# Panels for the large weights, and one 1024-column split per part in the mixture of experts (two transformer blocks, Trainium2, one core)

## The chip, the cores and the metric

The kernel runs on one core of one Trainium2 chip. The metric is the device time of one execution in microseconds (us). Engines are named as in the profile: PE multiplies matrices (PEld is its weight load), DVE and ACT are the vector and the scalar engine, POOL is GpSimd, SP issues most transfers. A form like `128x512` gives partitions x columns, and `out<-in` what an instruction writes and reads.

## What is computed

One sequence of 256 tokens with 1024 channels goes through two blocks in float32. Block 1 is an RWKV7 layer with a dense feed-forward part, then an attention layer with a mixture of 8 experts (two for each token, hidden width 3584). Block 2 has a mixer and a convolutional feed-forward part over 256 latent and 256 context tokens, and a second mixer with latent keys. The part that the change touches most:

```python
def swiglu(x, w_gate, w_up, w_down):
    return (jax.nn.silu(x @ w_gate) * (x @ w_up)) @ w_down

def moe_swiglu(x, router, w_gate, w_up, w_down):
    logits = (x @ router).astype(jnp.float32)
    top_logits, top_idx = lax.top_k(logits, TOP_K_EXPERTS)
    top_w = jax.nn.softmax(top_logits, axis=-1)
    gates = jnp.sum(jax.nn.one_hot(top_idx, N_EXPERTS, dtype=jnp.float32) * top_w[..., None], axis=-2)
...
    for e in range(N_EXPERTS):
        out = out + gates[..., e:e + 1] * swiglu(x, w_gate[e], w_up[e], w_down[e])
```

The weights of an expert are [1024, 3584] twice and [3584, 1024].

## The kernel before, in words

A product is held to float32 accuracy by splitting both operands into a high part (rounded to fp32r, which PE multiplies fast) and a low part (the rest): high x high, high x low and low x high are summed. A weight comes in **parts** of 128 partitions x 1024 float32 columns (512 KB). `wload` loads each part on SP's queue into a buffer `wraw` (6 of them), lets ACT copy it into `whi` and DVE subtract `whi` from `wraw` into `wlo` (4 buffers of each kind), both in pieces of `HI_N = LO_N = 512` columns. Each engine runs its instructions in one fixed order, which the framework's scheduler makes from the program, and waits at an instruction whose input isn't there. `act` is L242, `tt` L245, `stt` L254, `mm` L257, `tr` L277, the weights' transfer L301.

In the mixture of experts every expert runs over up to 128 of its tokens (`moe_experts`). A **block** is 512 hidden columns of one expert, 56 blocks in all. It has 12 parts: 4 of the gate's weight, 4 of up, and 4 of down (for the block before it). Each part is used in six matmuls of 512 columns, four with `whi` and two with `wlo`; `xg` are the tokens as stationary operand, `hT` the transposed hidden values. Between the parts stand:

- `gt` on ACT (tanh of the gate's sums, from PE), then `gs` twice on DVE (times the gate's sums, then times the up product's sums),
- four transposes of `gs` on PE (`ident,gs`), `hT` on ACT (their high part, from PE) and `hT` on DVE (their low part).

Where an expert ends its result is scaled (`yh`, `yl`) and scattered back (`moe_acc`); once for two experts the tokens are gathered (`xg`).

Before the change a row of gate or up lies in HBM as it is in the input: a part has for each partition two runs of 2048 bytes. A part of 256-column units (in `lin_T`) has four runs of 1024 bytes, and a part of down, or of another 1024-column matrix taken whole, one run of 4096.

Of the kernel before, what the change touches and what calls it, by code (L numbers as in the profile page):

```python
# [35 lines left out]
for _n, _k in VEC_SPECS:  # L36
# [3 lines left out]
# weight groups held for the last token tile; weights loaded before the lent tiles come in; transposed pairs whose  # L40
# scaling VectorE shares; columns per piece of a weight's split
# [7 lines left out]
    "x", "rwkv_w_rkv", "rwkv_w_out", "rwkv_decay_w0", "rwkv_decay_w1", "rwkv_decay_w2", "rwkv_iclr_a1",  # L49
    "rwkv_iclr_a2", "rwkv_gate_g1", "rwkv_gate_g2",  # L50
    "moba_w_k", "moba_w_v", "moba_w_q", "moba_w_o", "ffn_w_gate", "ffn_w_up", "ffn_w_down",
    "moe_router", "moe_w_gate", "moe_w_up", "moe_w_down", "ln_g", "ln_b",
    "ctx_2", "ada_w_2", "ffn_w_up_2", "ffn_w_down_2",
    "ev_w_in_2", "ev_gate_b_2", "ev_ml_norm_g_2", "ev_w_out_2",
    "od_w_dq_2", "od_w_uq_2", "od_w_dkv_2", "od_w_ukv_2", "od_w_o_2",
# [81 lines left out]
def pack(inputs):  # L137
    """Only layout: every vector that goes along partitions is laid out as [128, n]."""
    out = {}
    cols = []  # L140
    for n, k in VEC_SPECS:
        v = np.asarray(inputs[n], np.float32).reshape(k, P)
        cols.append(v.T)
    out["vecs"] = np.ascontiguousarray(np.concatenate(cols, 1))
    for n in RAW:
        out[n] = np.ascontiguousarray(np.asarray(inputs[n]))
    out["rpb"] = np.ascontiguousarray(np.asarray(inputs["ev_rpb_2"])[0].transpose(2, 0, 1))
    out.update(shape_consts()[0])
    return out
# [9 lines left out]
class Wt:  # L159
    """A weight unit on chip: k-tiles of [128, ncol], as high and low parts."""  # L160
# [16 lines left out]
class Act:  # L177
    """Activations with the contraction on partitions: k-tiles of [128, ntok], high and low parts."""
# [5 lines left out]
class Net:  # L184
    def __init__(self, ctx, tc, a):
        self.tc, self.nc, self.a = tc, tc.nc, a
# [11 lines left out]
        # tiles that the next weights are loaded into (None: one of their own)  # L198
# [60 lines left out]
    def mm3(self, out, xh, xl, wh, wl, start, stop):  # L259
        """One contraction step in float32 accuracy: hi*hi + hi*lo + lo*hi."""  # L260
        self.mm(out, xh, wl, start, False)
        self.mm(out, xl, wh, False, False)
        self.mm(out, xh, wh, False, stop)

    def mmk(self, out, ks, xh, xl, wh, wl, first, last):
        """Contraction steps ks in float32 accuracy, the products with the weights' high parts first; the
        activations are the stationary operand. first / last: the group's first and last steps."""
        for k in ks:
            self.mm(out, xh(k), wh(k), k == first, False)
            self.mm(out, xl(k), wh(k), False, False)  # L270
        for k in ks:
            self.mm(out, xh(k), wl(k), False, k == last)
# [6 lines left out]
    def split(self, hi, lo, src):  # L279
        """src as hi + lo, both readable by the fast float32 matmul."""  # L280
# [3 lines left out]
    def rpow(self, out, x, n, mul, add):  # L284
        """out = (x * mul + add) ** -0.5 for an [128, n] tile."""
# [5 lines left out]
    def wload(self, src, nk, ncol):  # L291
        """Loads [nk*128, ncol] by parts of at most 1024 columns of k-tiles and splits them."""
# [66 lines left out]
    def mmT(self, out, w, x, nk, w0, w1):  # L359
        """out [w1 - w0, 256] = w^T x over nk k-tiles, the weights being the stationary operand."""  # L360
# [6 lines left out]
    def lin_T(self, ch, x, nk, src, n, evac, mcol=P):  # L367
        """Channel-major output: for units of 256 columns evac(c0, ntiles, psum [128, ntiles, 256])."""
# [17 lines left out]
    def to_T(self, ch, src, x, nk=KD, scale=None, bias=None, f32=None):  # L386
        """src(tb) token-major [128, nk*128] -> x (channel-major hi/lo), optionally scaled and shifted per channel."""
# [34 lines left out]
    def layer_norm(self, h, gi, out):  # L422
        """In: h[tb] pre-norm sums [128,1024]; out(tb) normalised, ln_g/ln_b row gi = (layer, which)."""
# [154 lines left out]
def wkv(N, st, ch=0):  # L578
    """The delta-rule recurrence in chunks of 64 tokens, two heads (128 channels) at a time; three
    pairs are in flight: one prepares its products, one inverts, one walks over its chunks."""  # L580
# [151 lines left out]
    def walk(pr):  # L732
        # values with the two heads' tokens stacked on partitions
# [52 lines left out]
    def finish(pr):  # L786
        # group norm, bonus and gate; the result is channel-major
# [31 lines left out]
    # (stage, steps, start and length in units of a pair's turn)  # L819
# [11 lines left out]
def rwkv_out(N, st, ch=0):  # L831
    """Output projection, residual and layer norm."""
# [8 lines left out]
    yield from N.lin_tok(ch, x, KD, a["rwkv_w_out"][0], D, evac, late=lambda: None)  # L841
# [29 lines left out]
def ffn_parts(N, ch, x, wa, wg, parts, slots, unit, evac, wdown, late=None):  # L871
    """Runs unit(k, pa, pg, hi, lo) over pairs of 256 columns, then the down product, for each part of the hidden."""
# [20 lines left out]
def ffn_dense(N, st, ch=0):  # L893
    """SwiGLU feed-forward of block 1's first layer, residual and layer norm."""
# [19 lines left out]
    yield from ffn_parts(N, ch, x, a["ffn_w_gate"][0], a["ffn_w_up"][0], (12, 10), (4, 5, 6), unit, evac, a["ffn_w_down"][0],  # L914
# [20 lines left out]
def softmax_part(N, out, p, scale):  # L935
    """out = softmax(scale * p) along the free dimension."""
# [8 lines left out]
def turned(N, ch, S, n):  # L945
    """[128, n * 128] -> its n blocks transposed, for both heads."""
# [17 lines left out]
def moba(N, st, ch=0):  # L964
    """Block 1's attention layer: 256 tokens are one block, so all that stays is causal attention in it."""
# [15 lines left out]
    yield from paced(chain(N.lin_T(ch, x, KD, a["moba_w_q"][0], D, keep(qT)), N.lin_T(ch, x, KD, a["moba_w_k"], D, keep(kT)),  # L981
# [28 lines left out]
    def turn(pr):  # L1010
        # blocks: [keys0, q0], [keys0, q1], [keys1, q1]
# [18 lines left out]
    yield from paced(N.lin_tok(ch, o, KD, a["moba_w_o"][0], D, evac, late=lambda: None), SIDE["moba_out"])  # L1030
# [23 lines left out]
    # rank of each expert's logit (ties: the lower index first, as top_k)  # L1054
# [1001 lines left out]
```

## Time and profile before

| | |
|---|---|
| median of 3 runs | 2950.31 us (2949.16 to 2954.93) |
| span of the profiled execution | 2942.9 us, clock 0.976 (its whole time isn't given apart from the span) |
| PE busy | 2824.4 us, 96% |
| DVE busy | 2279.5 us, 77% |
| ACT busy | 1809.3 us, 61% |
| moved by transfers | 639.16 MB, 217 GB/s over the span |

The span goes from the first to the last instruction; the time also holds what lies around it. Busy time of matmuls is modelled at their ends, so a busy PE can still be waiting for a weight; the waits tell more. The mixture of experts takes about a third of the span, from some 943 to 1950 us. The stretch before it is the rest of block 1 with the parts of block 2 that don't depend on it, the stretch behind it block 2.

### The profile page before, as it was taken

How to read it: one execution, taken by the hardware profiler on the slowest of the kernel's cores; microseconds unless marked ns; L12 is line 12 of the kernel's file. 1: busy time of each engine (PE TensorE's matmuls, PEld its weight loads, DVE VectorE, ACT ScalarE, POOL GpSimd, SP SyncE). 2: the span in 40 equal slices, each digit the busy share in tenths (PEclk: the TensorE clock that was granted, in tenths of full speed). 3: DMA queues.
4: the chain of work that ended last, by engine and by line, in shares of the span. 5: the costliest groups of instructions: out<-in, count | busy, mean ns of one | idle time of the engine just before them, and what ended most of it. 6: DMA issues, size and time to landing. Idle time of an engine off the chain costs nothing. (4 is left out here: it accounts for less than half of the span.)

```text
span 2942.9 us, 46516 instructions
## 1 busy us (share of the span) xinstructions
PE 2824.4 (96%) x16596; PEld 2336.0 (79%) x16596; DVE 2279.5 (77%) x4406; ACT 1809.3 (61%) x3665; POOL 70.5 (2%) x96
## 2 busy tenths in 40 slices
PE   8999989999998999999999999979989999989898
PEld 8677779988866777778777777758978799877898
DVE  7455456568578999999999999977686786876767
ACT  5334345444466878787877878756444665666655
POOL 0001110000000000000000000000000000000000
PEclk9899989999999999999999999989989999999999
DMA  7346646654425999999999999965532356521463
GB/s 246 102 153 208 207 163 194 187 157 140 158 90 158 347 346 340 347 361 330 352 355 344 345 346 358 352 236 171 159 111 87 116 180 192 158 94 44 138 190 125
DMA packets 356247, 639.16 MB, mean 217 GB/s; under 512 B 25733, under 2 KB 152965, under 8 KB 356006
## 3 DMA queue, kind: packets, MB, share of 16 engines
q1 hardware_dynamic: 348768, 625.58, 63.2%
q10 hardware_dynamic: 7238, 10.52, 1.1%
q8 instruction: 133, 2.18, 0.3%
q14 instruction: 108, 0.88, 0.1%
HBM read 634.97 MB, written 1.05 MB: 216 GB/s over the span
## 5 line engine op out<-in xcount | busy, mean ns | idle before, releaser
L245 DVE TENSOR_TENSOR wlo<-wraw,whi 128x512 fp32r<-128x512 f32 (+1 forms) x2181 | 1377.4, 683 | 268.1 <-ACT whi L242 207.5
L242 ACT ACTIVATE whi<-wraw 128x512 fp32r<-128x512 f32 (+1 forms) x2181 | 1216.2, 621 | 452.7 <-PE ps L257 340.2
L257 PE MATMUL ps<-whi,xg 128*128 128x512 f32 x1792 | 498.7, 397 | 1.0 <-ACT whi L242 1.0
L257 PEld LDWEIGHTS ps<-whi,xg 128*128 128x128 f32 x1792 | 327.3, 188 | 84.7 <-ACT whi L242 23.6
L257 PE MATMUL ps<-wlo,xg 128*128 128x512 f32 x896 | 295.4, 398 | 0.0
L257 PE MATMUL ps<-whi,hT 128*128 128x512 f32 x896 | 259.9, 401 | 0.0
L257 PE MATMUL ps<-hT0h,whi 128*128 128x256 f32 (+2 forms) x872 | 215.3, 284 | 3.8 <-ACT whi L242 3.3
L257 PE MATMUL ps<-hT0l,whi 128*128 128x256 f32 (+2 forms) x872 | 215.1, 284 | 0.3 <-DVE hT0l L245 0.3
L257 PEld LDWEIGHTS ps<-wlo,xg 128*128 128x128 f32 x896 | 168.1, 188 | 55.7 <-DVE wlo L245 20.2
L257 PE MATMUL ps<-whi,hid 128*128 128x512 f32 x704 | 193.6, 411 | 9.6 <-DVE cv L254 3.7
L257 PEld LDWEIGHTS ps<-whi,hT 128*128 128x128 f32 x896 | 164.3, 188 | 33.3 <-ACT whi L242 0.6
L257 PEld LDWEIGHTS ps<-hT0h,whi 128*128 128x128 f32 (+2 forms) x872 | 167.0, 192 | 4.9 <-ACT whi L242 3.5
L257 PEld LDWEIGHTS ps<-whi,hid 128*128 128x128 f32 x704 | 133.6, 194 | 45.7 <-issue 13.4
L257 PEld LDWEIGHTS ps<-hT0l,whi 128*128 128x128 f32 (+2 forms) x872 | 167.1, 192 | 1.0 <-DVE hT0l L245 0.5
L257 PE MATMUL ps<-wlo,hT 128*128 128x512 f32 x448 | 167.5, 416 | 0.0
L257 PE MATMUL ps<-hT1h,whi 128*128 128x256 f32 (+1 forms) x504 | 127.9, 290 | 21.3 <-ACT whi L242 21.3
L254 DVE SCALAR_TENSOR_TENSOR cv<-ps,vecs,cv 128x255 f32<-128x255 f32 x264 | 124.6, 478 | 14.1 <-ACT cv L242 12.6
L257 PE MATMUL ps<-hT1l,whi 128*128 128x256 f32 (+1 forms) x504 | 125.9, 286 | 0.2 <-DVE hT1l L245 0.2
L257 PE MATMUL ps<-hT0h,wlo 128*128 128x256 f32 (+2 forms) x872 | 124.1, 283 | 1.6 <-DVE wlo L245 1.5
L257 PEld LDWEIGHTS ps<-hT0h,wlo 128*128 128x128 f32 (+2 forms) x872 | 112.8, 191 | 3.0 <-DVE wlo L245 2.6
L257 PEld LDWEIGHTS ps<-hT1h,whi 128*128 128x128 f32 (+1 forms) x504 | 96.3, 191 | 23.6 <-ACT whi L242 21.7
L257 PEld LDWEIGHTS ps<-wlo,hT 128*128 128x128 f32 x448 | 84.2, 188 | 28.4 <-DVE wlo L245 10.4
(539 smaller groups left out, 4708.6 us busy)
## 6 DMA issues: line engine op xcount, KB each, us to landing
wraw<-moe_w_down SPq DMA_DIRECT2D x224, 512.0 KB, 5.5
wraw<-moe_w_gate SPq DMA_DIRECT2D x222, 512.0 KB, 5.1
wraw<-moe_w_up SPq DMA_DIRECT2D x222, 512.0 KB, 5.5
wraw<-ffn_w_up SPq DMA_DIRECT2D x154, 512.0 KB, 4.0
wraw<-ada_w SPq DMA_DIRECT2D x96, 512.0 KB, 4.0
wraw<-ffn_w_down SPq DMA_DIRECT2D x88, 512.0 KB, 3.7
wraw<-ev_w_in SPq DMA_DIRECT2D x56, 512.0 KB, 3.7
wraw<-rwkv_w_rkv SPq DMA_DIRECT2D x24, 512.0 KB, 6.6
```

The costliest lines, as they stand in the source:

```text
L242: self.nc.scalar.activation(out, in_, f, **kw)
L245: (eng or self.nc.vector).tensor_tensor(out, x, y, op=op)
L254: (eng or self.nc.vector).scalar_tensor_tensor(out, x, s, y, op0=op0, op1=op1)
L257: self.nc.tensor.matmul(out, l, r, start=start, stop=stop)
```

## The change

Two things. First, the host lays out most large weights by **panels**: for each part the 1024 columns of a partition stand together, so that a part has one run of 4096 bytes for each partition (gate, up, the 256-column units, the 512-column units; down of the experts, `ada_w`, `od_w_uq`, `od_w_dkv` and `od_w_ukv` stay). `Pan` finds a part in such a panel. Second, `wload` takes the width of the pieces, and the experts' two calls ask for 1024: one instruction on ACT and one on DVE for each part, where there were two and two. Elsewhere the pieces stay at 512. (Comments and docstrings go too, which changes nothing.)

```diff
+def panel_width(w, nk):
+    return max(1, min(nk, 1024 // w))
+
+def panels(m, w):
+    nk, n = m.shape[0] // P, m.shape[1]
+    per = panel_width(w, nk)
+    m = m.reshape(nk // per, per, P, n // w, w)
+    return np.ascontiguousarray(m.transpose(3, 0, 2, 1, 4).reshape(n // w, nk // per, P, per * w))
+
+class Pan:
...
+    def part(self, k, m, ncol):
+        k += self.r0 // P
+        assert ncol == self.w and k % self.per == 0 and m <= self.per and self.c0 % self.w == 0
+        return self.ap[self.c0 // self.w, k // self.per][:, :m * ncol]
...
-    def wload(self, src, nk, ncol):
+    def wload(self, src, nk, ncol, hn=HI_N, ln=LO_N):
...
-            nc.sync.dma_start(raw[:, :m * ncol].rearrange("p (k c) -> p k c", k=m),
-                              src[k0 * P:(k0 + m) * P].rearrange("(k p) c -> p k c", p=P))
+            if isinstance(src, Pan):
+                nc.sync.dma_start(raw[:, :m * ncol], src.part(k0, m, ncol))
+            else:
+                nc.sync.dma_start(raw[:, :m * ncol].rearrange("p (k c) -> p k c", k=m),
+                                  src[k0 * P:(k0 + m) * P].rearrange("(k p) c -> p k c", p=P))
...
-            for q in range(0, m, HI_N):
-                e = min(q + HI_N, m)
+            for q in range(0, m, hn):
+                e = min(q + hn, m)
                 self.act(hi[:, q:e], r[:, q:e])
-            for q in range(0, m, LO_N):
-                e = min(q + LO_N, m)
+            for q in range(0, m, ln):
+                e = min(q + ln, m)
                 self.tt(lo[:, q:e], r[:, q:e], hi[:, q:e].bitcast(F32), ALU.subtract)
...
-                w = N.wload(wsrc[0, e, k0 * P:(k0 + 4) * P, f0:f0 + 512], 4, 512)
+                w = N.wload(wsrc[k0 * P:(k0 + 4) * P, f0:f0 + 512], 4, 512, 1024, 1024)
...
-            w = N.wload(a["moe_w_down"][0, e, f0 + j2 * 256:f0 + (j2 + 1) * 256, :], 2, D)
+            w = N.wload(a["moe_w_down"][0, e, f0 + j2 * 256:f0 + (j2 + 1) * 256, :], 2, D, 1024, 1024)
```

The new lines shift the numbers of those below: L242, L245, L254, L257, L277 and L301 become L292, L295, L304, L307, L327 and L352 (panels) or L354 (the rest).

ACT's order in a plain block of the experts, before: 12 half pieces stand between gt and hT, and 12 between hT and the next gt.

```order
L242 ACTIVATE gt<-ps 128x512
L242 ACTIVATE whi<-wraw 128x512 x12
L242 ACTIVATE hT_12851<-ps 128x512
L242 ACTIVATE whi<-wraw 128x512 x12
L242 ACTIVATE gt<-ps 128x512
```

The same place after the change:

```order
L292 ACTIVATE gt<-ps 128x512
L292 ACTIVATE whi<-wraw 128x1024 x6
L292 ACTIVATE hT_12379<-ps 128x512
L292 ACTIVATE whi<-wraw 128x1024 x6
L292 ACTIVATE gt<-ps 128x512
```

The 12 pieces are six whole ones; gt and hT stand after the same number of parts as before.

DVE's order in a plain block, before (`gs<-gt,ps` uses gt, `gs<-gs,ps` the up product's sums):

```order
L254 SCALAR_TENSOR_TENSOR gs<-gt,ps 128x512
L245 TENSOR_TENSOR wlo<-wraw,whi 128x512 x7
L254 SCALAR_TENSOR_TENSOR gs<-gs,ps 128x512
L245 TENSOR_TENSOR wlo<-wraw,whi 128x512 x5
L245 TENSOR_TENSOR hT_12852<-ps,hT_12851 128x512
L245 TENSOR_TENSOR wlo<-wraw,whi 128x512 x12
```

And after:

```order
L304 SCALAR_TENSOR_TENSOR gs<-gt,ps 128x512
L295 TENSOR_TENSOR wlo<-wraw,whi 128x1024 x4
L304 SCALAR_TENSOR_TENSOR gs<-gs,ps 128x512
L295 TENSOR_TENSOR wlo<-wraw,whi 128x1024 x2
L295 TENSOR_TENSOR hT_12380<-ps,hT_12379 128x512
L295 TENSOR_TENSOR wlo<-wraw,whi 128x1024 x6
```

The second gs stands after four whole parts, where it stood after three and a half; hT stands after six in both.

PE's order in the down product of a plain block, from its fifth matmul on, before: the transposes stand in two pairs, the second behind the eleventh matmul.

```order
L257 MATMUL ps<-wlo,hT_14049 128x512
L277 MATMUL ps<-ident,gs 128x128 x2
L257 MATMUL ps<-whi,hT_14049 128x512
L257 MATMUL ps<-whi,hT_14050 128x512
L257 MATMUL ps<-wlo,hT_14049 128x512
L257 MATMUL ps<-whi,hT_14049 128x512
L257 MATMUL ps<-whi,hT_14050 128x512
L257 MATMUL ps<-wlo,hT_14049 128x512
L277 MATMUL ps<-ident,gs 128x128 x2
L257 MATMUL ps<-wlo,hT_14049 128x512
L257 MATMUL ps<-whi,hT_14049 128x512
L257 MATMUL ps<-whi,hT_14050 128x512
```

And after, from the fifth matmul on:

```order
L307 MATMUL ps<-wlo,hT_13433 128x512 x2
L307 MATMUL ps<-whi,hT_13433 128x512
L307 MATMUL ps<-whi,hT_13434 128x512
L307 MATMUL ps<-whi,hT_13433 128x512
L307 MATMUL ps<-whi,hT_13434 128x512
L327 MATMUL ps<-ident,gs 128x128 x4
L307 MATMUL ps<-wlo,hT_13433 128x512 x2
L307 MATMUL ps<-whi,hT_13433 128x512
L307 MATMUL ps<-whi,hT_13434 128x512
```

The four transposes stand together, behind the tenth of the down product's 24 matmuls. In the experts' stretch the number of matmuls is the same; outside of it the rows of PE, DVE, ACT and POOL don't change but for line numbers.

## Rows read from the trace of the kernel before

**Rows 1.** Windows, experts: busy us (count) of PE, PEld, DVE, ACT, POOL; PEclk, DMA share, GB/s

```profile
1400.00:1450.00 50.00, 50.00 (x218) 38.62 (x218) 47.14 (x78) 40.65 (x76) 0.00 (x0) 1.00 0.99 361
```

**Rows 2.** Waits from 960 to 1900 us: total us, times, longest

```profile
ACT hT L242 <- PE ps L277: 87.6, 51, 2.9
ACT gt L242 <- PE ps L257: 65.0, 48, 1.9
PEld ps L257 <- DVE wlo L245: 29.0, 100, 0.4
...
PEld ps L257 <- ACT whi L242: 22.6, 86, 0.7
```

**Rows 3.** Tile gt: ns min/median/max, first and last start

```profile
L242 ACT ACTIVATE gt<-ps x56: 577/598/602, 942.6 to 1929.0; 128x512 f32<-128x512 f32 x56
```

**Rows 4.** Timeline of ACT, three gt in a row: start us, us, [idle before]

```profile
1424.40 0.60 ACT L242 ACTIVATE gt<-ps 128x512 f32<-128x512 f32 x1 [1.51 <-PE ps L257]
...
1441.95 0.60 ACT L242 ACTIVATE gt<-ps 128x512 f32<-128x512 f32 x1 [1.78 <-PE ps L257]
...
1460.70 0.60 ACT L242 ACTIVATE gt<-ps 128x512 f32<-128x512 f32 x1 [1.62 <-PE ps L257]
```

**Rows 5.** Timeline behind gt in a plain block, all engines

```profile
1406.95 0.60 ACT L242 ACTIVATE gt<-ps 128x512 f32<-128x512 f32 x1 [1.03 <-PE ps L257]
...
1407.44 1.14 ACT L242 ACTIVATE whi<-wraw 128x512 fp32r<-128x512 f32 x2
1407.58 0.69 DVE L254 SCALAR_TENSOR_TENSOR gs<-gt,ps 128x512 f32<-128x512 f32 x1 [0.66 <-ACT gt L242]
...
1408.12 0.30 PEld L257 LDWEIGHTS ps<-whi,xg 128*128 128x128 f32 x2 [0.27 <-ACT whi L242]
...
1408.19 2.64 DVE L245 TENSOR_TENSOR wlo<-wraw,whi 128x512 fp32r<-128x512 f32 x4
...
1409.53 0.19 PEld L257 LDWEIGHTS ps<-wlo,xg 128*128 128x128 f32 x1 [0.36 <-DVE wlo L245]
...
1409.86 0.62 PE L257 MATMUL ps<-whi,xg 128*128 128x512 f32 x2
```

**Rows 6.** Timeline behind hT in the same block

```profile
1415.83 0.60 ACT L242 ACTIVATE hT<-ps 128x512 fp32r<-128x512 f32 x1 [0.69 <-PE ps L277]
...
1416.33 3.75 ACT L242 ACTIVATE whi<-wraw 128x512 fp32r<-128x512 f32 x7
1416.46 0.69 DVE L245 TENSOR_TENSOR hT<-ps,hT 128x512 fp32r<-128x512 f32 x1
...
1417.04 0.89 PEld L257 LDWEIGHTS ps<-whi,hT 128*128 128x128 f32 x4
1417.07 3.09 DVE L245 TENSOR_TENSOR wlo<-wraw,whi 128x512 fp32r<-128x512 f32 x5
...
1418.41 0.19 PEld L257 LDWEIGHTS ps<-wlo,hT 128*128 128x128 f32 x1 [0.25 <-DVE wlo L245]
...
1418.75 1.08 PE L257 MATMUL ps<-whi,xg 128*128 128x512 f32 x4
```

**Rows 7.** Tile xm1h, the same two forms at 1024 columns: ns min/median/max

```profile
L242 ACT ACTIVATE xm1h<-xm x2: 1047/1048/1048, 25.5 to 29.7; 128x1024 fp32r<-128x1024 f32 x2
L245 DVE TENSOR_TENSOR xm1l<-xm,xm1h x2: 1209/1209/1209, 28.4 to 32.0; 128x1024 fp32r<-128x1024 f32 x2
```

**Rows 8.** Groups by form, 960 to 1900 us: busy us, mean ns | idle before

```profile
L245 DVE TENSOR_TENSOR wlo<-wraw,whi 128x512 fp32r<-128x512 f32 x1244 | 769.8, 683 | 10.2 <-ACT whi L242 9.1
L242 ACT ACTIVATE whi<-wraw 128x512 fp32r<-128x512 f32 x1246 | 680.7, 622 | 31.4 <-DMA wraw<-moe_w_gate 6.7 <-PE ps L257 5.9 <-DMA wraw<-moe_w_down 4.7
```

**Rows 9.** The page's transfers: KB each, us from issue to landing

```profile
wraw<-moe_w_down SPq DMA_DIRECT2D x224, 512.0 KB, 5.5
...
wraw<-moe_w_up SPq DMA_DIRECT2D x222, 512.0 KB, 5.5
```

**Rows 10.** Waits from 0 to 940 us, the high parts' for transfers

```profile
ACT whi L242 <- DMA wraw<-rwkv_w_rkv: 1.3, 2, 0.9
```

More of the change, by code (lines that the diff above doesn't have):

```diff
@@ L48, with __init__, __getitem__ @@
 RAW = [
-    "x", "rwkv_w_rkv", "rwkv_w_out", "rwkv_decay_w0", "rwkv_decay_w1", "rwkv_decay_w2", "rwkv_iclr_a1",
+    "x", "rwkv_decay_w0", "rwkv_decay_w1", "rwkv_decay_w2", "rwkv_iclr_a1",
     "rwkv_iclr_a2", "rwkv_gate_g1", "rwkv_gate_g2",
[L51 to L55, printed above, removed]
-]
+    "moe_router", "moe_w_down", "ln_g", "ln_b",
+    "ctx_2", "ada_w_2", "ev_gate_b_2", "ev_ml_norm_g_2",
+    "od_w_uq_2", "od_w_dkv_2", "od_w_ukv_2",
+]
+PANELS = [
+    ("p_r", "rwkv_w_rkv", (0, 0), (0, 1024), 256), ("p_k", "rwkv_w_rkv", (0, 1), (0, 1024), 256),
+    ("p_v", "rwkv_w_rkv", (0, 2), (0, 1024), 512), ("rwkv_w_out", "rwkv_w_out", (0,), (0, 1024), 512),
+    ("moba_w_q", "moba_w_q", (0,), (0, 1024), 256), ("moba_w_k", "moba_w_k", (), (0, 1024), 256),
+    ("moba_w_v", "moba_w_v", (), (0, 1024), 512), ("moba_w_o", "moba_w_o", (0,), (0, 1024), 512),
+    ("ffn_w_gate", "ffn_w_gate", (0,), (0, 2816), 256), ("ffn_w_up", "ffn_w_up", (0,), (0, 2816), 256),
+    ("ffn_w_down", "ffn_w_down", (0,), (0, 1024), 512),
[8 rows of a table added]
+]
+for _n in ("moe_w_gate", "moe_w_up"):
+    PANELS += [(f"{_n}{e}", _n, (0, e), (0, FFE), 512) for e in range(NE)]
+def panel_width(w, nk):
[6 more added lines that the diff above has]
+class Pan:
+    def __init__(self, ap, w, nk, r0=0, c0=0):
+        self.ap, self.w, self.nk, self.per, self.r0, self.c0 = ap, w, nk, panel_width(w, nk), r0, c0
+    def __getitem__(self, s):
+        r, c = s if isinstance(s, tuple) else (s, slice(None))
+        return Pan(self.ap, self.w, self.nk, self.r0 + (r.start or 0), self.c0 + (c.start or 0))
+    def part(self, k, m, ncol):
+        k += self.r0 // P
+        assert ncol == self.w and k % self.per == 0 and m <= self.per and self.c0 % self.w == 0
+        return self.ap[self.c0 // self.w, k // self.per][:, :m * ncol]
 def shape_consts():
@@ L146, in pack @@
         out[n] = np.ascontiguousarray(np.asarray(inputs[n]))
+    for n, src, i, (c0, c1), w in PANELS:
+        out[n] = panels(np.asarray(inputs[src])[i][:, c0:c1], w)
     out["rpb"] = np.ascontiguousarray(np.asarray(inputs["ev_rpb_2"])[0].transpose(2, 0, 1))
@@ L185, in __init__ @@
     def __init__(self, ctx, tc, a):
-        self.tc, self.nc, self.a = tc, tc.nc, a
+        self.tc, self.nc, self.a = tc, tc.nc, dict(a)
+        for n, _, _, _, w in PANELS:
+            self.a[n] = Pan(a[n], w, a[n].shape[1] * (a[n].shape[3] // w))
         ep = ctx.enter_context
@@ L840, in evac @@
         N.stt(o, o, ALPHA, p[:, :ncol], ALU.mult, ALU.add)
-    yield from N.lin_tok(ch, x, KD, a["rwkv_w_out"][0], D, evac, late=lambda: None)
+    yield from N.lin_tok(ch, x, KD, a["rwkv_w_out"], D, evac, late=lambda: None)
     N.layer_norm(lambda tb: h[:, tb * D:(tb + 1) * D], (0, 0), lambda tb: h[:, tb * D:(tb + 1) * D])
@@ L913, in evac @@
             N.tt(o, o, p[:, :ncol], ALU.add)
-    yield from ffn_parts(N, ch, x, a["ffn_w_gate"][0], a["ffn_w_up"][0], (12, 10), (4, 5, 6), unit, evac, a["ffn_w_down"][0],
+    yield from ffn_parts(N, ch, x, a["ffn_w_gate"], a["ffn_w_up"], (12, 10), (4, 5, 6), unit, evac, a["ffn_w_down"],
                          lambda: None)
@@ L980, in vevac @@
         N.act(v[:, tb * D + c0:tb * D + c0 + ncol], p[:, :ncol])
-    yield from paced(chain(N.lin_T(ch, x, KD, a["moba_w_q"][0], D, keep(qT)), N.lin_T(ch, x, KD, a["moba_w_k"], D, keep(kT)),
+    yield from paced(chain(N.lin_T(ch, x, KD, a["moba_w_q"], D, keep(qT)), N.lin_T(ch, x, KD, a["moba_w_k"], D, keep(kT)),
                            N.lin_tok(ch, x, KD, a["moba_w_v"], D, vevac)), SIDE["moba_in"])
@@ L1029, in evac @@
         N.stt(q, q, ALPHA, p[:, :ncol], ALU.mult, ALU.add)
-    yield from paced(N.lin_tok(ch, o, KD, a["moba_w_o"][0], D, evac, late=lambda: None), SIDE["moba_out"])
+    yield from paced(N.lin_tok(ch, o, KD, a["moba_w_o"], D, evac, late=lambda: None), SIDE["moba_out"])
     N.layer_norm(lambda tb: h[:, tb * D:(tb + 1) * D], (1, 0), lambda tb: h[:, tb * D:(tb + 1) * D])
@@ L1423, in evac @@
             N.tt(o, o, p[:, :ncol], ALU.add)
-    up = a["ffn_w_up_2"][l]
+    up = a[f"ffn2_up{l}"]
     row = []
-    yield from ffn_parts(N, ch, x, up[:, 0:FF], up[:, FF:2 * FF], parts, hslots, unit, evac, a["ffn_w_down_2"][l],
+    yield from ffn_parts(N, ch, x, up[:, 0:FF], up[:, FF:2 * FF], parts, hslots, unit, evac, a[f"ffn2_down{l}"],
                          lambda: row.extend(gate_row(N, st, ch, l, 1, r)))
@@ L1475, in even_proj @@
     nc, a = N.nc, N.a
-    w = a["ev_w_in_2"][0]
     qo = N.slot(S["qo"], f"nq_mlo{ch}")
@@ L1507, in conv @@
         N.ts(o, o, 0.5 * (128.0 ** -0.5 if k < 4 else 1.0))
-    yield from N.lin_T(ch, x, KD, w[:, 1536:2560], 1024, conv)
-    wg = N.wload(w[:, 3584:3600], KD, 16)
+    yield from N.lin_T(ch, x, KD, a["ev_qk"], 1024, conv)
+    wg = N.wload(a["ev_g"], KD, 16)
     gb = N.sm(1, "gateb")
@@ L1902, in evac @@
         N.act(ql.rearrange("p (n t) -> p n t", n=2), p)
-    yield from paced(N.lin_T(ch, x, KD, N.a["od_w_dq_2"][0], 256, evac), pace)
+    yield from paced(N.lin_T(ch, x, KD, N.a["od_w_dq_2"], 256, evac), pace)
     lat = mla_down(N, ch, x)
```

25 lines of the change are left out of this document (12 added, 13 removed), and 8 rows, old and new, of the table PANELS.

## The prediction

> **What bounds the kernel now.** I read the profile from coarse to fine: the page, the windows of 50 us, the groups of instructions by form, the waits, and then the timeline of one block, where the waits can be put in order.
>
> The page says that PE is busy for 96% of the span. The weights of the experts (the stretch from about 943 to 1950 us) are where the change alters instructions, so I read that stretch by itself. In a window of it all four resources look full [rows 1]: PE busy 50 of 50 us, DVE 47.1, ACT 40.7, the DMA engines at a share of 0.99 with 361 GB/s. Any of them could pass for the bound, and the shares do not decide it. The waits do [rows 2]. In 940 us ACT waits 87.6 us for the transposes ahead of hT and 65.0 us for the gate's sums ahead of gt: it stands idle for PE, it is not late. PE's weight loads wait 29.0 us for DVE's low parts (100 times) and 22.6 us for ACT's high parts (86 times), about 1 us in each of the 52 blocks of that window. So PE is the bound of a block, and what it loses, it loses to hand-overs at two places, not to a full engine.
>
> The block is the unit of the sum. gt runs once in a block, 56 times from 942.6 to 1929.0 us [rows 3], a mean distance of 986.4 / 55 = 17.93 us. Listing all 55 distances I count 35 of 17.6 us or less ("plain" below) and 20 of 18.65 to 19.99, in which an expert's result is combined or the next pair's tokens are gathered. One of each: 17.55 us from 1424.40, 18.75 us from 1441.95 [rows 4].
>
> **The first place, behind gt** [rows 5]. ACT is idle 1.03 us until PE ends the gate's sums, runs gt at 1406.95, and only then goes on to the high part of the next weight part: two 512-column pieces from 1407.44, 1.14 us for both, so the first is there at about 1408.06. PE's load takes it at 1408.12, after 0.27 us of waiting. DVE runs gs (from 1407.58) and begins the low pieces at 1408.19; PE waits 0.36 us for the second and loads it at 1409.53; PE's next part begins at 1409.86. **The second place, behind hT** [rows 6]. ACT waits 0.69 us for the transposes, runs hT at 1415.83, high pieces from 1416.33, 7 in 3.75 us. PE loads the first at 1417.04, with no wait. DVE's low pieces start at 1417.07, behind its own hT (1416.46); PE waits 0.25 us for the second at 1418.41, and the next part begins at 1418.75. At both places the pieces are handed on by halves, and PE starts on the first half while the second is being made.
>
> **The change, part by part.**
>
> (a) One instruction for a part. A 128x1024 copy to fp32r on ACT takes 1048 ns and a subtraction of this form on DVE 1209 ns [rows 7], against 622 and 683 ns for the halves [rows 8]. Seen as work this saves. Back to back, ACT's 7 pieces in 3.75 us are (3.75 - 0.62) / 6 = 0.522 us each and DVE's 5 in 3.09 us are (3.09 - 0.68) / 4 = 0.602 each [rows 6], so that a part costs 1.04 and 1.20 us; if the long forms overlap their neighbours by as much (0.10 and 0.08 us, an estimate), a part will cost 0.95 and 1.13. That is 0.08 us of DVE a part, 0.9 us in a block of 12, some 50 us over 672 parts. It is worth nothing where the engine then waits for PE, as both do in every block.
>
> Seen as a hand-over it costs. The first half no longer comes after 0.62 us; nothing comes before 1.05 us, and DVE can't start while ACT is on the second half. At the first place: ACT starts at 1407.44 as before, because gt stands after the same number of parts in its order; the whole high part is there at 1408.49, and PE's load goes at 1408.54 instead of 1408.12. DVE's subtraction starts at about 1408.55 instead of 1408.19 and ends 1.21 later, at 1409.76. In the rows a load follows its piece by some 0.06 us, so the first low load goes at 1409.82. From the second low load to the next part it is 0.33 us in the rows (1409.53 to 1409.86), and the first load lies one matmul ahead of that, 0.23 us (50 us over 218 in the window of [rows 1]): the next part begins 0.56 us behind it, at 1410.38 instead of 1409.86: **+0.52 us**.
>
> At the second place the same chain gives 1416.33 + 1.05 = 1417.38 for the high part, 1417.44 + 1.21 = 1418.65 for the low, 1418.71 + 0.34 + 0.23 = 1419.28 for the next part instead of 1418.75: +0.53, if hT stays where it is. It does not: PE's order after the change has the four transposes together behind ten of the down product's 24 matmuls, where the last pair stood behind eleven, so hT can start 0.23 us earlier against PE, and ACT, which waited 0.69 us there, can use all of it: **+0.30 us**. The ends are 0.53, if DVE's queue or gs keeps hT where it is, and 0, if ACT and DVE, having gained on PE at the first place, bring hT further forward still. A plain block then costs 0.82 us more (0.52 to 1.05); 35 of them 29 us (18 to 37).
>
> In the other 20 blocks other work on PE, one to two microseconds of it (the distances), lies among the parts and can cover a late hand-over. The nearest rows are the plain blocks at one end and no cost at the other: 0 to 1.05 us each, 0 to 21 us. I take +0.2 each, 4 us, because the extra instructions stand on ACT's and DVE's queues as well and delay them by about what they give PE.
>
> The Trainium skill weighs both sides of this edit in one section ("Perfetto Trace Analysis", Optimizing Scalar/DVE Operations): larger operations improve throughput if the engine is saturated, and if engines are not saturated but cause bubbles on others, "breaking up instructions may allow work to be completed sooner". By the first half the edit would gain, by the second it loses; the idle 1.03 and 0.69 us put this kernel into the second.
>
> (b) Panels. Gate and up weights now come in 4096-byte runs for each partition, as the down weights always have. From issue to landing a part of up takes 5.5 us in its 2048-byte runs and a part of down 5.5 us in its 4096-byte runs [rows 9]: the row shows nothing to be had from longer runs here. ACT waited for gate and down transfers 6.7 and 4.7 us in 940 us [rows 8], and behind such waits PE mostly had parts in hand. So 0, with 11.4 us as the most. Outside of the experts the order of PE, DVE, ACT and POOL is unchanged row by row, and the only wait of a high part for a weight is 1.3 us at the start [rows 10]: -1 us, with 0 and -1.3 as ends. Fewer packets on SP's queue delay nobody: no instruction moves past another there.
>
> **Sum.** 29 + 4 + 0 - 1 = +32 us. The view shows one execution's span, 2942.9 us; the median of the runs is 2950.31, 7.4 us more, which lies around the span and which I leave as it is. 2942.9 + 32 = 2974.9 of span, 2950.3 + 32 = **2982 us**, 1.1% slower. Its own ends are 18 - 11 - 1 = +6 and 37 + 21 = +58 us, 2956 to 3008; both need all unknowns on one side, so I count 2964 to 3002 as its range. What a measurement of this kernel can tell from no change is 0.2%, 5.9 us.
>
> **Rivals.**
>
> *DVE and ACT set the pace after all.* If a block of 12 parts were bound by DVE (12 x 1.20 + 3 x 0.61 for gs, gs and hT = 16.3 of 17.5 us), the saved 0.9 us would show, up to the 1 us that PE waits: half of it in 55 blocks is -25 us, **2925 us**. For it speaks DVE's 47.1 of 50 us; against it the 0.66 us that DVE stands idle for gt ahead of gs in the very block [rows 5], and that 12 x 0.08 us can't be used before the gate's sums are done. 0.06.
>
> *The transfers set the pace.* A block needs 12 x 512 KB = 6.29 MB, at 361 GB/s 17.4 us, just what it takes. If longer runs freed ACT's waits, 11.4 us go: **2939 us**. For it: the share of 0.99. Against it: the equal landing times, and a queue that is full because SP issues whenever a buffer comes free. The Trainium skill ("Perfetto Trace Analysis", DMA Optimizations) says that going from 2 KB to 4 KB transfers can improve throughput dramatically when DMA-bound; by it this rival would hold. 0.05.
>
> *The buffers swallow it.* Four high and four low buffers let ACT and DVE run ahead of PE; if they were two parts ahead at each place, the late first half would be covered and the time stay at **2950 us**. It decides itself by how many parts stand between the wait for PE and PE's need: at the first place it is one (six matmuls, 1.4 us), which gt, one long copy and one long subtraction (0.5 + 1.05 + 1.21) exceed. 0.07.
>
> **How the numbers follow.** Slower by the hand-over 0.82, no change 0.07, transfers 0.05, engines 0.06. Faster is 0.11, the same 0.07, slower 0.82. The time is that of the likeliest. The range takes the likeliest's own and reaches down to the case of no change: 2950 to 3002; it leaves out the two faster cases and the likeliest's tails, together under 2 in 10.
>
> **What would show it.** gt to gt in plain blocks 18.2 to 18.5 us instead of 17.5; whi 1048 and wlo 1209 ns, 672 of each; PE's loads waiting in the same stretch some 80 to 95 us for ACT and DVE instead of 52, at the first part behind gt and behind hT; the DMA share down to about 0.94 with unchanged bytes; the stretches before 940 us as they were. Wrong it would be if plain blocks stay at 17.5 (the buffers), or fall toward 16.8 with ACT's waits for transfers or DVE's for nothing gone; a gain before 940 us would show that I priced the panels too low.

## The result, and the profile after

The changed kernel takes 2981.82 us (median of 4 runs, 2978.59 to 2986.0) beside 2952.62 us for the kernel before: a ratio of 1.0105, 95% interval 1.0088 to 1.0122. 2982 was forecast, inside a range of 2950 to 3002. The span of the profiled execution is 2976.8 us, 33.9 us longer than before, at the same clock of 0.976.

The window of 50 us that stood ahead of the prediction [rows 1], now of the kernel after (busy us and count of PE, PEld, DVE, ACT, POOL; PEclk, DMA share, GB/s):

```profile
1400.00:1450.00 50.00, 48.88 (x211) 37.48 (x211) 43.77 (x42) 34.26 (x38) 0.00 (x0) 1.00 0.93 342
```

211 matmuls where there were 218. DVE and ACT have less to do (43.8 and 34.3 us), the transfers are less dense (0.93 and 342 GB/s), and PE, which was busy for the whole window, is so for 48.9 us and gets less done: everything has more room but the hand-over. The waits from 960 to 1930 us, again about 52 blocks (total us, times, longest):

```profile
ACT hT L292 <- PE ps L327: 114.6, 49, 3.2
ACT gt L292 <- PE ps L307: 97.7, 48, 2.9
...
PEld ps L307 <- DVE wlo L295: 44.1, 90, 0.7
PEld ps L307 <- ACT whi L292: 36.0, 88, 0.7
DVE wlo L295 <- ACT whi L292: 35.0, 118, 1.0
...
PE ps L307 <- ACT whi L292: 9.4, 36, 0.3
```

The waits of PE's loads for split weights were 51.6 us [rows 2]; the two rows here make 80.1, and with the wait of the matmuls themselves it is 89.5. ACT and DVE wait longer for PE than before, so the saved work turned into idle time. DVE waiting for the high part, 35.0 us, was 9.1 [rows 8]: it has to stand by while ACT makes the half it doesn't need yet. gt in the experts (first and last start), and three of them on ACT's timeline:

```profile
L292 ACT ACTIVATE gt<-ps x56: 578/600/604, 945.4 to 1963.3; 128x512 f32<-128x512 f32 x56
```

```profile
1422.54 0.60 ACT L292 ACTIVATE gt<-ps 128x512 f32<-128x512 f32 x1 [2.62 <-PE ps L307]
...
1440.76 0.60 ACT L292 ACTIVATE gt<-ps 128x512 f32<-128x512 f32 x1 [2.77 <-PE ps L307]
...
1459.01 0.60 ACT L292 ACTIVATE gt<-ps 128x512 f32<-128x512 f32 x1 [1.62 <-PE ps L307]
```

From first to last it is 1017.96 us instead of 986.41: +31.5 of the +33.9 lie between them. A plain block takes 18.22 to 18.25 us here, 17.45 to 17.55 before [rows 4].

The first place, behind the gt at 1440.76 (timeline of all engines), to be held against [rows 5]:

```profile
1441.26 3.89 ACT L292 ACTIVATE whi<-wraw 128x1024 fp32r<-128x1024 f32 x4
1441.39 0.69 DVE L304 SCALAR_TENSOR_TENSOR gs<-gt,ps 128x512 f32<-128x512 f32 x1 [1.23 <-ACT gt L292]
...
1442.34 2.36 DVE L295 TENSOR_TENSOR wlo<-wraw,whi 128x1024 fp32r<-128x1024 f32 x2 [0.25 <-ACT whi L292]
1442.36 0.76 PEld L307 LDWEIGHTS ps<-whi,xg 128*128 128x128 f32 x4 [0.70 <-ACT whi L292]
...
1443.62 0.30 PEld L307 LDWEIGHTS ps<-wlo,xg 128*128 128x128 f32 x2 [0.49 <-DVE wlo L295]
...
1444.19 0.39 PE L307 MATMUL ps<-whi,xg 128*128 128x512 f32 x1
```

From gt to the start of PE's next part it is 1444.19 - 1440.76 = 3.43 us; before it was 1409.86 - 1406.95 = 2.91. PE's load waits 0.70 us for the high part, then 0.49 for the low one, where the waits were 0.27 and 0.36: **+0.52 us**, the forecast's figure. The second place, behind hT, to be held against [rows 6]:

```profile
1431.68 0.60 ACT L292 ACTIVATE hT<-ps 128x512 fp32r<-128x512 f32 x1 [1.58 <-PE ps L327]
...
1432.17 3.89 ACT L292 ACTIVATE whi<-wraw 128x1024 fp32r<-128x1024 f32 x4
...
1433.26 2.36 DVE L295 TENSOR_TENSOR wlo<-wraw,whi 128x1024 fp32r<-128x1024 f32 x2 [0.26 <-ACT whi L292]
1433.28 0.76 PEld L307 LDWEIGHTS ps<-whi,hT 128*128 128x128 f32 x4 [0.20 <-ACT whi L292]
...
1434.54 0.30 PEld L307 LDWEIGHTS ps<-wlo,hT 128*128 128x128 f32 x2 [0.50 <-DVE wlo L295]
...
1435.11 0.62 PE L307 MATMUL ps<-whi,xg 128*128 128x512 f32 x2
```

3.43 us from hT to the next part, 2.92 before: +0.51 counted from hT. The whole block grew by 18.22 - 17.45 = 0.77, so after +0.52 at the first place 0.25 is left for the second: hT comes 0.26 us earlier against PE. The distances between the two say the same: from gt to hT it was 1415.83 - 1406.95 = 8.88 us and is now 9.14, only 0.26 more, and from hT to the next gt it was 8.57 and is now 9.08, the 0.51. The two new forms (mean ns) and two rows of transfers (KB, us from issue to landing):

```profile
L295 DVE TENSOR_TENSOR wlo<-wraw,whi 128x1024 fp32r<-128x1024 f32 x623 | 728.9, 1221 | 36.4 <-ACT whi L292 35.0 <-PE ps L307 0.3
L292 ACT ACTIVATE whi<-wraw 128x1024 fp32r<-128x1024 f32 x623 | 622.7, 1054 | 38.7 <-DMA wraw<-moe_w_down 10.4 <-PE ps L307 9.6 <-DMA wraw<-moe_w_gate 6.5
```

```profile
wraw<-moe_w_down SPq DMA_DIRECT2D x224, 512.0 KB, 5.4
...
wraw<-moe_w_up SPq DMA_DIRECT2D x222, 512.0 KB, 5.3
```

1054 and 1221 ns, as the two other tiles had shown [rows 7]. Up lands after 5.3 us in its 4096-byte runs and took 5.5 in 2048-byte ones [rows 9]; gate, with the same change of layout, lands after 5.2 and took 5.1, and down, which didn't change, 5.4 and 5.5, so these differences are of the size of the scatter.

### The profile page after: what moved, and what is told of

It reads as the page before. It is cut to its first block, busy times and chain, and to the rows that moved or that the text cites. A ratio compares the mean times of both kernels' runs of the same rounds, so it can differ in the third digit from the quotient of the medians.

```text
span 2976.8 us, 45225 instructions
## 1 busy us (share of the span) xinstructions
PE 2840.0 (95%) x16596; PEld 2340.8 (79%) x16596; DVE 2246.9 (75%) x3734; ACT 1748.4 (59%) x2993; POOL 69.6 (2%) x96
## 3 DMA queue, kind: packets, MB, share of 16 engines
HBM read 634.97 MB, written 1.05 MB: 214 GB/s over the span
## 5 line engine op out<-in xcount | busy, mean ns | idle before, releaser
L295 DVE TENSOR_TENSOR wlo<-wraw,whi 128x512 fp32r<-128x512 f32 (+2 forms) x1513 | 1333.0, 920 | 300.0 <-ACT whi L292 235.0
L292 ACT ACTIVATE whi<-wraw 128x512 fp32r<-128x512 f32 (+2 forms) x1513 | 1153.6, 812 | 459.1 <-PE ps L307 348.0
L307 PE MATMUL ps<-whi,xg 128*128 128x512 f32 x1792 | 491.5, 396 | 9.9 <-ACT whi L292 9.9
L307 PEld LDWEIGHTS ps<-whi,xg 128*128 128x128 f32 x1792 | 331.7, 188 | 100.4 <-ACT whi L292 28.9
L307 PE MATMUL ps<-wlo,xg 128*128 128x512 f32 x896 | 284.1, 398 | 2.5
L307 PE MATMUL ps<-whi,hT 128*128 128x512 f32 x896 | 246.8, 397 | 0.0
L307 PE MATMUL ps<-hT0h,whi 128*128 128x256 f32 (+2 forms) x872 | 215.6, 285 | 3.8 <-ACT whi L292 3.3
L307 PE MATMUL ps<-hT0l,whi 128*128 128x256 f32 (+2 forms) x872 | 215.5, 284 | 0.3 <-DVE hT0l L295 0.3
L307 PEld LDWEIGHTS ps<-wlo,xg 128*128 128x128 f32 x896 | 162.4, 188 | 53.6 <-DVE wlo L295 21.6
L307 PE MATMUL ps<-whi,hid 128*128 128x512 f32 x704 | 190.5, 406 | 10.9 <-DVE cv L304 4.1
L307 PEld LDWEIGHTS ps<-whi,hT 128*128 128x128 f32 x896 | 164.9, 188 | 45.0 <-ACT whi L292 9.1
L307 PEld LDWEIGHTS ps<-hT0h,whi 128*128 128x128 f32 (+2 forms) x872 | 167.3, 192 | 4.9 <-ACT whi L292 3.5
L307 PEld LDWEIGHTS ps<-hT0l,whi 128*128 128x128 f32 (+2 forms) x872 | 167.4, 192 | 1.1 <-DVE hT0l L295 0.5
L307 PEld LDWEIGHTS ps<-whi,hid 128*128 128x128 f32 x704 | 131.5, 191 | 46.1 <-issue 13.9
L307 PE MATMUL ps<-wlo,hT 128*128 128x512 f32 x448 | 149.9, 416 | 4.7 <-DVE wlo L295 1.9
L307 PE MATMUL ps<-hT1h,whi 128*128 128x256 f32 (+1 forms) x504 | 132.5, 297 | 19.5 <-ACT whi L292 19.5
L304 DVE SCALAR_TENSOR_TENSOR cv<-ps,vecs,cv 128x255 f32<-128x255 f32 x264 | 124.9, 478 | 14.1 <-ACT cv L292 12.6
L307 PE MATMUL ps<-hT1l,whi 128*128 128x256 f32 (+1 forms) x504 | 130.2, 293 | 0.2 <-DVE hT1l L295 0.2
L307 PE MATMUL ps<-hT0h,wlo 128*128 128x256 f32 (+2 forms) x872 | 124.5, 285 | 1.1 <-DVE wlo L295 1.0
L307 PEld LDWEIGHTS ps<-hT1h,whi 128*128 128x128 f32 (+1 forms) x504 | 99.9, 198 | 22.2 <-ACT whi L292 20.2
L307 PEld LDWEIGHTS ps<-hT0h,wlo 128*128 128x128 f32 (+2 forms) x872 | 113.6, 192 | 2.2 <-DVE wlo L295 1.7
L292 ACT ACTIVATE hT<-ps 128x512 fp32r<-128x512 f32 x56 | 33.5, 598 | 122.1 <-PE ps L327 122.1
```

Of the source, the lines that this page charges most:

```text
L292: self.nc.scalar.activation(out, in_, f, **kw)
L295: (eng or self.nc.vector).tensor_tensor(out, x, y, op=op)
L304: (eng or self.nc.vector).scalar_tensor_tensor(out, x, s, y, op0=op0, op1=op1)
L307: self.nc.tensor.matmul(out, l, r, start=start, stop=stop)
```

## Experiments

The theory: the loss comes from handing on whole parts at the two places where ACT and DVE, held up by PE's sums, have just one part of PE's work as cover; the layout and the amount of work on ACT and DVE have no share in it. Rivals: the transfers, the throughput of the engines, and the wide forms by themselves. Every ratio is to the kernel before on the same chip. Some of the edits change the scheduler's order too: in the experts `panels_only` has PE's, ACT's and DVE's order of before and `wide_only` that of after; for others it is said where it matters. The blocks named plain below are the 30 distances of gt from the sixth on that were 17.6 us or less before; their mean was 17.49 us before and is 18.27 after.

**Panels without the wide pieces** (`panels_only`):

```diff
-                w = N.wload(wsrc[k0 * P:(k0 + 4) * P, f0:f0 + 512], 4, 512, 1024, 1024)
+                w = N.wload(wsrc[k0 * P:(k0 + 4) * P, f0:f0 + 512], 4, 512, 512, 512)
...
-            w = N.wload(a["moe_w_down"][0, e, f0 + j2 * 256:f0 + (j2 + 1) * 256, :], 2, D, 1024, 1024)
+            w = N.wload(a["moe_w_down"][0, e, f0 + j2 * 256:f0 + (j2 + 1) * 256, :], 2, D, 512, 512)
```

> Panels as in the change, but the experts' parts split in 512-column pieces again. Every engine's order is then that of before. Theory (the hand-over of a whole part costs, the layout nothing): 2950 to 2953 us, plain blocks 17.45 to 17.6 us, PE's loads waiting about 52 us in the experts. Rival (the new transfers or their source cost something in the experts): plain blocks above 17.7 us and the time toward 2965 or more. The first gt came 2.8 us later after the change; if the panels are the reason it does so here too.

2945.55 us, a little below the 2950 to 2953 expected; ratio 0.999 (0.9976 to 1.0004); plain blocks 17.48 us. The layout alone can't be told from no change. At the start rT, the first product's result, begins at 23.9 us, and at 25.0 in the kernel before (two rows of ACT, before and with panels; first and last start):

```profile
L242 ACT ACTIVATE rT<-ps x4: 573/577/580, 25.0 to 40.7; 128x512 f32<-128x512 f32 x4
```

```profile
L292 ACT ACTIVATE rT<-ps x4: 575/576/577, 23.9 to 39.5; 128x512 f32<-128x512 f32 x4
```

That would be the microsecond of the forecast, but one pair of executions doesn't show it: in the ten profiled executions with panels rT begins between 23.6 and 25.5 us, in the three with the old layout between 25.0 and 26.5. gt comes first at 941.75 us here, so its 2.8 us of delay in the profile after isn't the panels'.

**The wide pieces in the old layout** (`wide_only`), the kernel before with the new arguments of `wload` and

```diff
-                w = N.wload(wsrc[0, e, k0 * P:(k0 + 4) * P, f0:f0 + 512], 4, 512)
+                w = N.wload(wsrc[0, e, k0 * P:(k0 + 4) * P, f0:f0 + 512], 4, 512, 1024, 1024)
...
-            w = N.wload(a["moe_w_down"][0, e, f0 + j2 * 256:f0 + (j2 + 1) * 256, :], 2, D)
+            w = N.wload(a["moe_w_down"][0, e, f0 + j2 * 256:f0 + (j2 + 1) * 256, :], 2, D, 1024, 1024)
```

> Layout of before, the experts' parts split in one 1024-column instruction on ACT and one on DVE. Theory: as the change, 2980 to 2985 us, plain blocks 18.2 to 18.4 us. Rival (panels and width both carry a share): in between, near 2966 us.

2980.48 us, ratio 1.0108 (1.0088 to 1.0128); plain blocks 18.28 us, PE's loads waiting as in the changed kernel. The whole loss is the width's.

**Only the low part whole** (`hi512_lo1024`) and **only the high part whole** (`hi1024_lo512`), with panels; the calls' last two arguments become, for the first and the second,

```diff
-4, 512, 1024, 1024)
+4, 512, 512, 1024)
...
-4, 512, 1024, 1024)
+4, 512, 1024, 512)
```

> Panels; ACT's high part in halves, DVE's low part whole. By the chain the low part is the later one at both places: DVE must wait for both halves (0.52 + 0.62 = 1.14 us, against 1.05 whole), so halving the high part alone brings nothing: 18.2 to 18.5 us for a plain block, 2980 to 2988 us. Rival (PE waits for the high part first): most of the loss comes back, 2955 to 2965 us.

> Panels; ACT's high part whole, DVE's low part in halves. DVE starts 0.36 us late at both places but hands on by halves, so PE's next part is late by 0.36 to 0.37 us at each, 0.73 a plain block without the transposes' earlier place (PE's order is that of before here): about 18.1 us, 2970 to 2978 us. Rival (only DVE's width matters): 2950 to 2956 us.

2989.19 us, ratio 1.0137 (1.0117 to 1.0157), and 2978.34 us, ratio 1.0102 (1.0082 to 1.0123), a shade above what was expected of each; plain blocks 18.48 and 18.22. Halving only the first step of the chain is worse than not halving at all: the interval of its ratio overlaps a little with those of the kernels with both whole, but its plain blocks, 18.40 to 18.55 us, all lie above theirs, 18.19 to 18.38. PE's waits with only the low part whole (waits from 960 to 1930 us here, and in the next rows):

```profile
PEld ps L307 <- DVE wlo L295: 61.5, 133, 1.0
DVE wlo L295 <- ACT whi L292: 48.2, 117, 1.2
...
PEld ps L307 <- ACT whi L292: 24.5, 74, 0.5
```

ACT's first half lets PE begin early (24.5 us of waits, 36.0 with both whole), but DVE needs both halves, which take longer than one whole copy, and PE pays at the low part (61.5). With only the high part whole it is the other way round:

```profile
PEld ps L307 <- ACT whi L292: 45.0, 89, 0.7
PEld ps L307 <- DVE wlo L295: 33.7, 94, 1.0
```

Each width costs its own step, and the two don't add up: the whole loss is there with either one. Nor is the new place of the transposes on PE, which came with the wide pieces, needed for a loss: with only the high part whole they stand in two pairs as before, and a plain block still loses 0.74 us on average, shared by the two places (one block: from gt to hT 9.22 us, to the next gt 8.93; before 8.88 and 8.57):

```profile
1401.72 0.60 ACT L292 ACTIVATE gt<-ps 128x512 f32<-128x512 f32 x1 [1.10 <-PE ps L307]
...
1410.94 0.60 ACT L292 ACTIVATE hT<-ps 128x512 fp32r<-128x512 f32 x1 [2.51 <-PE ps L327]
...
1419.87 0.60 ACT L292 ACTIVATE gt<-ps 128x512 f32<-128x512 f32 x1 [1.71 <-PE ps L307]
```

**gt later, wide pieces kept** (`gt_later_wide`). The first five distances of gt after the change are 0.00 to 0.27 us longer than before, the next ones 0.85 to 0.94. Counted in ACT's order, gt stands two to four parts behind the gate's in these first blocks, and from then on one (two in the second block of each expert's end, after the change). In the first blocks ACT isn't late but ahead, waiting for PE to free a buffer (ACT in the third block of the kernel after):

```profile
975.44 0.58 ACT L292 ACTIVATE gt<-ps 128x512 f32<-128x512 f32 x1
975.91 1.05 ACT L292 ACTIVATE whi<-wraw 128x1024 fp32r<-128x1024 f32 x1
977.26 1.06 ACT L292 ACTIVATE whi<-wraw 128x1024 fp32r<-128x1024 f32 x1 [0.29 <-PE ps L307]
```

So gt is put behind the third part of up everywhere, two parts later than in a plain block (`his`, which `wload` now fills, holds the last copy of each part; `issue_after` makes the scheduler queue what is inside it behind the instruction named):

```diff
-        N.act(t, ws[0], AF.Tanh, scale=0.5)
+        with N.tc.issue_after(N.his[-2].ins):
+            N.act(t, ws[0], AF.Tanh, scale=0.5)
```

> The changed kernel (panels, 1024-column pieces) with gt queued on ACT behind the third part of up instead of the first; nothing else is forced. Theory (one part between the wait for PE and PE's need is too little for a whole-part hand-over; the first blocks, in which gt stands two or more parts later, lost nothing): the loss at the first place goes and the old waits there with it, plain blocks 17.4 to 17.7 us, 2948 to 2962 us. Rival (wide instructions cost by themselves, or DVE is late behind the later gs): plain blocks stay at 18.2 us, 2975 us or more.

2950.66 us, ratio 1.0014 (1.0004 to 1.0024); plain blocks 17.52 us on average. Nearly all of the loss is gone with the wide pieces in place. ACT no longer waits for PE at gt (1.0 us in all, 97.7 before this edit), and PE's loads wait 43.1 instead of 80.1 us (waits from 960 to 1900 us, again about 52 blocks):

```profile
PEld ps L308 <- DVE wlo L296: 29.7, 64, 0.7
...
PEld ps L308 <- ACT whi L293: 13.4, 55, 0.9
...
ACT gt L293 <- PE ps L308: 1.0, 2, 0.8
```

**hT later alone** (`hT_later_wide`), the changed kernel with

```diff
-        N.split(hT[0], hT[1], pt)
+        with N.tc.issue_after(N.his[-1].ins):
+            N.split(hT[0], hT[1], pt)
```

> The changed kernel with hT alone queued one part later on ACT and DVE, gt left one part behind the gate's. Theory by the chain: the second place's loss (0.25 to 0.3 us a plain block) and its old wait go, the first place's 0.5 stays: plain blocks 17.7 to 18.0 us, 2962 to 2974 us. Rival: all of the loss stands behind gt, 2978 us or more.

2963.94 us, ratio 1.005 (1.0031 to 1.007); plain blocks 17.85 to 18.02. From gt to hT a plain block keeps the 9.14 us of the changed kernel, and from hT to the next gt it takes 8.72 instead of 9.08: the move gives back at the second place alone. **Both** (`both_later_wide`):

> As the run before, and hT on ACT and DVE queued behind the last part of the down product. Theory: no hand-over stands within one part of PE any more, plain blocks like the first ones of before (17.15 to 17.25 us), 2932 to 2945 us, faster than before in spite of the wide pieces. Rival: the second place isn't a cost of its own, same time as the run before; or later hT delays gs and the next block, slower than it.

2933.47 us, ratio 0.9943 (0.9931 to 0.9956), faster than the kernel before with the very pieces that made it slower. The distances of gt wander here (plain ones 16.15 to 18.02 us, 16.94 on average, where 17.15 to 17.25 was expected), so the whole stretch says more. The two moves nearly add: from the changed kernel's ratio of 1.0105 the one takes 0.0091, the other 0.0055, both 0.0162. **Both with halves** (`both_later_halves`), the same two edits on `panels_only`:

> The same two moves with panels and 512-column pieces. Theory: where the hand-over is covered the width of the pieces doesn't matter: within 0.3% of the run before. Rival (DVE's or ACT's work counts once PE no longer waits): slower than the wide one by up to 0.9 us a block, 50 us.

2926.17 us, ratio 0.993 (0.9916 to 0.9943): the lowest median of all, though its interval overlaps with that of the wide one. Where the hand-over is covered the width makes 0.13%, if anything, and not 1.05; PE's transposes stand together with the wide pieces and in two pairs with the halves, which may have a share in that difference. From the first gt of the experts to the last it is 970.8 us with wide pieces and 969.6 with halves, and was 986.4 before (first and last start, wide and halves):

```profile
L293 ACT ACTIVATE gt<-ps x56: 577/582/603, 945.2 to 1916.0; 128x512 f32<-128x512 f32 x56
L293 ACT ACTIVATE gt<-ps x56: 576/580/599, 944.2 to 1913.8; 128x512 f32<-128x512 f32 x56
```

**One part less of delay for gt** (`both_later_gt_one_less`):

```diff
-        with N.tc.issue_after(N.his[-2].ins):
+        with N.tc.issue_after(N.his[-3].ins):
             N.act(t, ws[0], AF.Tanh, scale=0.5)
```

> Panels, 512-column pieces, hT one part later, gt behind the second part of up instead of the third. Theory: two parts between are cover enough for halves (0.5 + 0.62 + 0.68 us against 2.7 us of PE), and DVE's gs comes sooner, so that buffers come free sooner and fewer waits for transfers arise: 2918 to 2928 us. Rival: the cover is too thin again, 2930 us or more.

2931.04 us, ratio 0.9941 (0.9921 to 0.996): above the 2918 to 2928 expected and not to be told from the one before; the hoped-for gain isn't there.

**The old layout where transfers count most** (`both_later_old_layout`): the same two edits on the kernel before. In `both_later_halves` PE's loads hardly wait for splits, and what comes up instead is ACT waiting for transfers (waits from 960 to 1900 us):

```profile
ACT whi L293 <- DMA wraw<-moe_w_down: 21.5, 38, 1.5
...
ACT whi L293 <- DMA wraw<-moe_w_gate: 19.5, 26, 1.6
...
ACT whi L293 <- DMA wraw<-moe_w_up: 15.8, 33, 1.5
...
PEld ps L308 <- DVE wlo L296: 10.3, 35, 0.4
```

> The layout of before (2048-byte runs for gate and up), 512-column pieces, gt and hT queued later as in both_later_halves: every engine has the same order as there, only the runs of the transfers differ. There ACT waits for transfers some 58 us in the experts, so if longer runs are ever worth something it is here. Theory (parts of both layouts land equally fast): within 0.3%, 2922 to 2934 us. Rival (2048-byte runs are slower once transfers are next to the bound): 2940 us or more.

2929.44 us, ratio 0.9925 (0.9907 to 0.9942): the same, and ACT waits as long for transfers (58 us from 960 to 1930 us, 59 with panels). Runs of 4096 bytes instead of 2048 bring nothing measurable even there.

**Pieces of 256** (`pieces_256`), with panels:

```diff
-4, 512, 1024, 1024)
+4, 512, 256, 256)
...
-2, D, 1024, 1024)
+2, D, 256, 256)
```

> Panels, pieces of 256 columns on both engines. If only the hand-over counted it would gain on before (first piece 0.2 us earlier), about 2940 us. But DVE's 256-column form takes some 0.42 us (0.34 back to back, by the fixed share seen at 512), 1.38 us a part, 16.6 us a block and 18.4 with gs, gs and hT: DVE becomes the bound and plain blocks take 18.3 to 18.6 us, 2990 to 3010 us. The order that the scheduler makes differs in places too.

2982.94 us, ratio 1.0108 (1.0092 to 1.0124); plain blocks 18.16 us, both below what was expected (2990 to 3010 and 18.3 to 18.6). This is the case in which an engine does set the pace (window of the kernel with 256-column pieces, where DVE is the third pair of numbers, and the largest wait from 960 to 1930 us):

```profile
1450.00:1500.00 50.00, 48.77 (x204) 35.52 (x202) 49.77 (x139) 43.41 (x135) 0.00 (x0) 1.00 0.94 329
```

```profile
PEld ps L307 <- DVE wlo L295: 67.8, 187, 1.1
```

DVE is busy 49.8 of 50 us (49.6 on average from 1000 to 1950 us, 46.9 in the kernel before) and PE waits for the low part. One of DVE's chains of 28 such pieces took 9.47 us:

```profile
1450.59 9.47 DVE L295 TENSOR_TENSOR wlo<-wraw,whi 128x256 fp32r<-128x256 f32 x28
```

With 0.42 us for one, that is (9.47 - 0.42) / 27 = 0.335 us apiece, 1.34 a part; with the three others (gs, gs and hT, 0.61 each as in the prediction) a block needs 17.9 us of DVE.

## Why the prediction was right, step by step

**The bound of a block** was read rightly from the waits and not from the shares. Four resources were near full, and of these the transfers and DVE were cleared by `panels_only`, `both_later_old_layout` and `both_later_halves`: the last two are faster than the kernel before with the same bytes and the same pieces. The hand-overs were 1 us a block before and 1.7 after.

**The first place, +0.52 us**: measured +0.52, by the same chain. The estimate of what a wide piece takes back to back (0.95 and 1.13 us) holds too: four on ACT took 3.89 us and two on DVE 2.36, 0.95 and 1.14 for each further one.

**The second place, +0.30 us**: measured +0.25 net, +0.51 behind hT less 0.26 for the transposes' earlier place (0.23 forecast). In `hi1024_lo512`, where they stand as before, nothing of this kind is gained: from gt to hT it is 0.34 us longer, where the chain gave 0.36 for that edit.

**35 plain blocks, +29 us**: measured +23.9. The size of one block was right (0.79 on average for the 30, 0.70 to 0.89, where 0.82 was forecast), but the first five lose nothing or little, since gt stands further back in ACT's order there. The rival of the buffers holds in these blocks: ACT is ahead, and the late first half is covered. I had given its deciding point (how many parts stand between the wait and the need) and not looked whether it is the same in all blocks.

**The other 20 blocks, +4 us**: measured +7.6, from -0.32 to +0.94 a block. At an expert's end without a gather the first of two such blocks loses 0.6 to 0.9 us and the second next to nothing; with a gather it is 0.9, 0.5, -0.3 and 0.2 to 0.4 in a row. In the first of them the extra work on PE covers nothing: in the 3.5 us behind gt PE's loads wait mostly some 0.85 us for split weights before and 1.19 after, as in a plain block. In the second they wait for none behind gt in either kernel; after the change gt stands two parts behind the gate's there and not one. Why something is won where tokens are gathered, no run takes apart. The two misses, -5 and +4, cancel in the sum; that it came out so close is in part luck.

**Panels in the experts 0, at the start -1 us**: 0.999 (0.9976 to 1.0004); the microsecond at the start is within the scatter of rT and isn't shown. The 11.4 us given as the most counted the wait for down, whose layout stays; for gate and up ACT waited 6.7 and 2.2 us. In the profiled execution after, the first gt came 2.8 us late all the same; it came at 941.75 with panels and at 948.0 in a run with the old layout (`both_later_old_layout`), and in the other kernels in between, so this is the scatter between executions.

**The throughput rival** fell twice: DVE's 0.9 us a block saved nothing while PE's waits held it up, and between wide pieces and halves there is no gain for the wide ones when little holds it up. It holds at 256 columns. **The transfer rival** fell with `panels_only` and `both_later_old_layout`: the two layouts take the same time, even with 57 us of waits for transfers in the experts. The one rule that spoke for it, the Trainium skill's on 2 KB and 4 KB transfers ("Perfetto Trace Analysis", DMA Optimizations), is not borne out by any run here; it is said of DMA-bound work, and that any of these kernels is DMA-bound no run shows either. The Trainium skill's other rule ("Perfetto Trace Analysis", Optimizing Scalar/DVE Operations), on breaking up instructions of an engine that isn't saturated but makes bubbles, describes what happened, 2950 us with halves and 2982 with whole parts; `pieces_256`, 2983 us with DVE busy 49.8 of 50 us, shows where its condition ends.

What stays open is what bounds `both_later_halves`. ACT's waits for transfers are the largest that a weight meets there, PE's loads wait 12 us in all for split weights, and whether the transfers could be started earlier wasn't tried.

## What to carry to other kernels

A producer that isn't the bound should be asked how long its consumer waits for the first piece, not how much it does in all: look for the place in its order where it is held up by the consumer itself, count what work the consumer has in hand from there, and compare it with the chain of the pieces. Where that cover is thin, moving the instruction that holds the producer up (here gt and hT, by two parts and one) was worth more than any width: -1.6% with the wide pieces, -0.7% against the kernel before. In a chain of two producers, halving only the first can make it worse.

## What the runs showed that was not expected

The prediction had not asked which half of the edit costs. Two half copies on ACT (1.14 us from the start of the first to the end of the second) take longer than a whole one (1.05), and halves of the high part with whole low parts gave the slowest kernel of all, 2989 us; that it would bring nothing was expected before that run, not that it would be worse. And the number of parts between the wait and the need, which the prediction had only as the deciding point of a rival, is worth more than the width: with gt and hT queued later both widths are faster than the kernel before.
